# A decoder step on one core: the gate's norm on VectorE, prompt queries and keys in groups of four token tiles, and the latents of two quads loaded later

## The chip, the core and the metric

The kernel runs on one core of a Trainium2 chip, as one launch. The metric is the device time of an execution in microseconds. Matmuls run on TensorE (PE), with weight loads shown apart (PEld); the other engines are VectorE (DVE), ScalarE (ACT), GpSimd (POOL) and SyncE (SP), which issues nearly all the DMAs.

## What is computed

One layer of a hybrid decoder, for a prompt of 1024 tokens and for 8 samples of 4 tokens each whose past of 4096 tokens lies in pages. The part that the change touches:

```python
u, v, cq, ckv, kpe = split_in(rms_norm(xp, g_mix) @ w_in)
# the gate: layer norm over 64 channels, then a causal 128x128 matrix per group
vg = layer_norm(gelu(v).reshape(n, t // c, c, 8, 64), ln_g, ln_b)
a_out = gelu(u) * (einsum('gts,nmsgd->nmtgd', w, vg) + b_s)
# queries and keys of the prompt: 8 heads of 64 + 32 rotated channels
q = qk_rope(rms_norm((rms_norm(cq, g_q_a) @ w_uq).reshape(n, t, 8, 96), g_qk_q), pos)
k = qk_rope(rms_norm(concat([ckv_n @ w_uk, kpe], -1), g_qk_k), pos)
b_out = masked_attend(q, k, ckv_n @ w_uv)
# the samples do the same against their paged latents
xp = xp + concat([rms_norm(a_out), rms_norm(b_out)], -1) @ w_o
```

Cross-attention into 256 memory tokens and a gated ConvFFN follow. All is in fp32.

## The kernel before

The 1056 token rows (1024 of the prompt, 32 of the samples) are nine tiles: 0 to 7 of 128 rows, and 8 of 32. Every fp32 product is made of three matmuls on a high and a low part (`mm3`, L180); `split` (L187) makes the parts, the high one by a cast on ACT and the low one by a subtraction on DVE (L191, L192, and L195, L198 with a gain). `rsqrt_steps` (L216 to L236) is a chain of 11 small DVE operations.

The stages, with their times in the profiled execution:

- *Phase 1, 0 to about 181 us.* The combined projection, in two halves of 256 channels. In each half the gate's values go through gelu on ACT (L457), mean, squares and `rsqrt` on DVE, then three products: by the reciprocal root on DVE (L468), and by the gain and plus the bias on POOL (L470, L472, and L475 for the samples' tile). The result is split into `vgh` and `vgl`, from which TensorE makes the gate. `wsc` (L410) is a copy of a corner of the gate's matrices. The latents `cq` and `ckv` follow in three column groups (`ckr` is the raw latent, `ckh` and `ckl` its parts; `ck_tok`, L576, holds the row scale), and `mix` normalises two tiles of the gate's output at a time, transposes them (L1540), copies them from PSUM (L1541) and stores them (L1543).
- *Projections, about 181 to 209.* `phase2a` first makes tables of cosines and sines times gains, and the rotated shared key `kr`, on POOL (`rope_tables`, `rope_tok`). Then `proj_group` makes queries, keys and values of the first four heads, two tiles at a time: copies and squares on ACT (L842 to L848, the values at L838), the norm on DVE (L849 to L862), the rotation of the queries on POOL (L600 to L603), the product of the keys with their norm on DVE (L871) and of the shared rotated part on POOL (L872). The squares' tiles are `hsq`, the norms `hr`.
- *Attention of the prompt, about 209 to 428.* `head_prep` transposes a head's queries and keys (L895) into `tp` and splits them into `kTh`, `kTl`, `qTh`, `qTl`. `head_unit` does scores (`s`), the eviction with mask and maximum on DVE (L922, L926, tile `pr` or `prs`), the exponential on ACT (L932), transposes (L941), a copy on ACT (`pth`, L943) and the product with the values (L953). The second four heads' projections are spread between these units: `late` groups with the steps given at L692 to L696. POOL sums weights in between (L793 to L796). Three `mix` steps of the attention's output run near the end (L716 to L731); their copies go into tiles of the ring `v`.
- *Samples, about 430 to 875.* Eight batches of eight quads, a quad being four pages. `quad_load` (L1226) reads page numbers into SP's registers and issues four DMAs of `cT` (the latents transposed, with the rope key; L1241; here called the quad's keys) and four of `ck` (the latents by token; L1245). `cT` has three buffers, `ck` fifteen. Quads 0 to 2 get their `cT` during the attention, and their `ck` at the start of this stage. `quad_rot` (L1258 to L1260) rotates the key on POOL; `ch` (ACT) and `cl` (POOL or DVE, L1273) are the parts. `quad_sums` squares the rope part of `ck`. `steps` (L1139) places all this by a counter n, two per quad.
- *From about 875:* keys and values of the memory, the output projection, memory attention, and from 1185 the ConvFFN.

What sets the order: up to the attention a scheduler orders each engine's instructions when the program is built; from the attention on, the order of PE, ACT, DVE and POOL is that of the code (`manual_schedule`). Each engine runs its instructions in order, so an instruction that waits holds up all behind it. SP's queue is in order as well.

## Time and profile before

| | us |
|---|---|
| three runs | 1867.88, 1870.19, 1870.91 |
| median of the runs | 1870.19 |
| the profiled execution | 1868.82 |
| its span | 1867.1 |
| TensorE busy | 1822.4 |
| TensorE idle over the span | 44.7 |

A row of the waits view names the engine and the instruction that waited, then what released it, then the total, the count and the longest. A row of a timeline has the start, the duration, the engine, the line, the operation, the tiles with their shapes, and in brackets the idle time before it and what ended that. A time in brackets on a row of several instructions belongs to the first.

### The profile page before, as it was taken

The page shows a single profiled execution, that of the slowest core. Times are in us where ns is not written, and L with a number is a line of the kernel's source. Part 1 is how long each engine was busy: PE and PEld are TensorE (multiplying, and loading weights), DVE is VectorE, ACT ScalarE, POOL GpSimd, SP SyncE. Part 2 cuts the span into 40 slices and gives each one's busy share as a digit, 9 for nine tenths or more (in the row PEclk, how much of TensorE's full clock was granted, in tenths as well). Part 3 has the DMA queues.
Part 4 walks back from the last instruction along what each step waited for, and adds up shares of the span by engine and source line. Part 5 has one row for each costly group of instructions (what it writes and reads, how often), then busy time and mean ns, then how long its engine had stood idle before and what let it go on. Part 6 is the DMA issues. An engine that isn't in the chain of part 4 may idle for free.

```text
span 1867.1 us, 39819 instructions
## 1 busy us (share of the span) xinstructions
PE 1822.4 (98%) x14414; PEld 1754.4 (94%) x14414; DVE 1376.8 (74%) x2873; ACT 927.6 (50%) x1965; POOL 712.1 (38%) x826
## 2 busy tenths in 40 slices
PE   9999899989999999999999999999999999999999
PEld 8899799889999999998899988899999999999999
DVE  7855967765777667876644676888888888879664
ACT  7335676666556555555533456533323333344442
POOL 1321415643444444543313110267776677500000
PEclk9999899999999999999999999999999999999999
DMA  8002205566776666664554345412222222495252
GB/s 329 29 15 78 68 1 193 205 228 185 220 207 189 175 177 189 170 177 147 163 165 130 127 159 157 136 58 86 76 92 81 69 79 71 117 349 170 75 154 76
DMA packets 133639, 260.18 MB, mean 139 GB/s; under 512 B 20545, under 2 KB 74658, under 8 KB 130370
## 3 DMA queue, kind: packets, MB, share of 16 engines
q1 hardware_dynamic: 132578, 256.58, 44.1%
q8 instruction: 114, 1.87, 0.4%
q10 hardware_dynamic: 864, 1.05, 0.2%
q14 instruction: 83, 0.68, 0.1%
HBM read 212.27 MB, written 45.30 MB: 138 GB/s over the span
## 4 chain that ended last, share of the span: by engine, by line
PE 64%; issue 4%; DVE 3%; DMA 2%; POOL 2%; SPq 1%; ACT 1%; POOLq 0%; DVEq 0%; ACTq 0%
PE s L185 14%; PE d L185 12%; PE b L185 7%; PE X L185 7%; PE F L185 7%; PE E L185 7%; PE A L185 3%; PE y L185 3%; DMA cT<-cT 1%; PE o L1388 1%; SPq L1241 1%; PE t L185 1%; POOL cl L1273 1%; DMA ck<-ck 1%; DVE ss L1316 1%
## 5 line engine op out<-in xcount | busy, mean ns | idle before, releaser
L185 PE MATMUL s<-w2h,ch 128*128 128x288 f32 (+1 forms) x1024 | 304.3, 297 | 0.0
L185 PE MATMUL s<-w2h,cl 128*128 128x288 f32 (+1 forms) x1024 | 296.6, 290 | 3.6 <-POOL cl L1273 3.6
L185 PE MATMUL s<-w2l,ch 128*128 128x288 f32 (+1 forms) x1024 | 295.3, 288 | 0.0
L185 PEld LDWEIGHTS s<-w2h,ch 128*128 128x128 f32 x1024 | 193.2, 189 | 8.3 <-issue 2.9
L185 PEld LDWEIGHTS s<-w2h,cl 128*128 128x128 f32 x1024 | 193.1, 189 | 5.5 <-POOL cl L1273 5.4
L185 PEld LDWEIGHTS s<-w2l,ch 128*128 128x128 f32 x1024 | 193.5, 189 | 0.0
L1316 DVE TENSOR_REDUCE ss<-sq 128x16 f32<-128x1024 f32 x128 | 155.3, 1214 | 34.0 <-ACT sq L1313 33.6
L1273 POOL TENSOR_TENSOR cl<-cT,ch 128x512 fp32r<-128x512 f32 x64 | 83.3, 1301 | 113.9 <-ACT ch L1269 101.6
L1313 ACT ACTIVATE sq<-s 128x512 f32<-128x512 f32 x128 | 76.5, 598 | 91.5 <-PE s L185 91.4
L1310 ACT ACTIVATE sq<-s 128x512 f32<-128x512 f32 x128 | 76.7, 599 | 72.6 <-PE s L185 72.2
L191 ACT CAST a<-brb 128x528 fp32r<-128x528 f32 x77 | 48.9, 635 | 110.7 <-PE d L185 105.4
L192 DVE TENSOR_TENSOR a<-brb,a 128x528 fp32r<-128x528 f32 x77 | 54.2, 706 | 56.7 <-ACT a L191 56.6
L185 PE MATMUL d<-a,w 128*128 128x264 f32 x768 | 95.4, 284 | 0.4 <-DVE G L2108 0.4
L185 PEld LDWEIGHTS d<-a,w 128*128 128x128 f32 x768 | 94.3, 188 | 0.6 <-issue 0.6
L953 PEld LDWEIGHTS o<-v,pth 128*128 128x128 f32 x576 | 75.8, 197 | 7.4 <-ACT pth L943 5.2
L953 PE MATMUL o<-v,pth 128*128 128x64 f32 x576 | 76.2, 274 | 4.8 <-ACT pth L943 4.4
L1979 POOL TENSOR_TENSOR lo<-s,hi 128x1024 fp32r<-128x1024 f32 x20 | 62.9, 3143 | 45.7 <-ACT hi L1978 45.7
L185 PE MATMUL mm<-whi,xh 128*128 128x256 f32 (+3 forms) x272 | 77.9, 288 | 0.0
L185 PE MATMUL mm<-wlo,xh 128*128 128x256 f32 (+3 forms) x272 | 77.7, 288 | 0.0
L185 PE MATMUL mm<-whi,xl 128*128 128x256 f32 (+3 forms) x272 | 77.3, 288 | 0.0
L2034 ACT COPY a<-A 128x264 f32<-128x264 f32 x43 | 16.1, 375 | 118.8 <-PE A L185 113.9
L1269 ACT CAST ch<-cT 128x512 fp32r<-128x512 f32 x128 | 73.4, 626 | 0.8 <-DMA cT<-cT 0.8
(737 smaller groups left out, 6480.6 us busy)
## 6 DMA issues: line engine op xcount, KB each, us to landing
cT<-cT SPq DMA_DIRECT2D x256, 160.0 KB, 2.8
ck<-ck SPq DMA_DIRECT2D x256, 144.0 KB, 3.5
raw<-w_up SPq DMA_DIRECT2D x44, 512.0 KB, 3.6
wsumd<-wsum SPq DMA_DIRECT2D x13, 1024.0 KB, 4.5
actd<-cv SPq DMA_DIRECT2D x44, 264.0 KB, 2.4
brb<-actd SPq DMA_DIRECT2D x44, 264.0 KB, 5.7
wsum<-w_down SPq DMA_DIRECT2D x11, 1024.0 KB, 4.8
raw<-wsumd SPq DMA_DIRECT2D x20, 512.0 KB, 3.8
```

Source lines behind the costliest of these rows:

```text
L185: self.nc.tensor.matmul(out, l, r, start=first and i == 0, stop=last and i == len(seq) - 1)
L191: {"act": nc.scalar.copy, "pool": nc.gpsimd.tensor_copy, "dve": nc.vector.tensor_copy}[eng](hi, src)
L192: low = lambda: nc.vector.tensor_tensor(lo, src, hi, ALU.subtract)
L953: nc.tensor.matmul(u["o"][:, e], th[:, z * P : z * P + P], s["v"][:, jj, h % 4], start=j == z == 0, stop=e == 1 and jj == 2 * G + 1)
L1241: dmas.append([nc.sync.dma_start(cT[:, j], I["cT"][bass.ds(rv, 1)].rearrange("a p n -> (a p) n")) for j, rv in enumerate(rvs)])
L1269: nc.scalar.copy(d["h"][:, k], src[k])
L1273: (nc.vector if k else nc.gpsimd).tensor_tensor(d["l"][:, k], src[k], d["h"][:, k], ALU.subtract)
L1310: nc.scalar.activation(sq[:, 0], ps[:, :, n0 : n0 + 256], AF.Square)
L1313: nc.scalar.activation(sq[:, 1], pt.rearrange("p (e d) -> p e d", e=2), AF.Square)
L1316: yield lambda: nc.vector.tensor_reduce(s["ss"][:, g0 : g0 + 2].rearrange("p e (z h) -> p z e h", z=2), sq.rearrange("p z e (h d) -> p z e ...
L1388: nc.tensor.matmul(s["o"][j * 32 : j * 32 + 32], S[:, q * 4 + j], d["ck"][:, j, :257], start=q == 0 and j > 0, stop=q == 7)
L1979: eng.tensor_tensor(lo, src, hi, ALU.subtract)
```

## The change

1. Gate's norm: the copy at L410 and the products at L470, L472 and L475 go from POOL to DVE.
2. `mix` in phase 1 takes four tiles at a time (0 to 3 in one group; 4 to 7 and 8 in the next), scales the tile in place, and stores two tiles with one DMA. The three `mix` steps of the attention use tiles of the rings `k` and `q` instead of `v`.
3. The tables, the squares of the shared key and its rotation become `rope_setup`, called in phase 1 ahead of the loads of `w_uq`; `rope_tables` goes away.
4. `proj_group` runs on groups (0,4), (4,8), (8,9). Its norm works on four tiles at once; the rotation still goes by pairs. The pieces of the three groups are emitted in a new interleaving, and the late groups have other steps.
5. In `steps`, `ck` of quad 0 is loaded at n = -6, `ck` of quads 1 and 2 at n = 1 and n = 3, behind the loads of quads 3 and 4. `quad_sums` of quads 1 and 2 comes three steps later.

```diff
-            nc.gpsimd.tensor_copy(wsc, ws[:, :, :ND])
+            nc.vector.tensor_copy(wsc, ws[:, :, :ND])
...
-                    nc.gpsimd.tensor_tensor(gf, gf, lng[:tn, c0 : c0 + 256], ALU.mult)
+                    nc.vector.tensor_tensor(gf, gf, lng[:tn, c0 : c0 + 256], ALU.mult)
                     if i < 8:
-                        nc.gpsimd.tensor_tensor(gf, gf, lnb[:tn, c0 : c0 + 256], ALU.add)
+                        nc.vector.tensor_tensor(gf, gf, lnb[:tn, c0 : c0 + 256], ALU.add)
...
+        self.rope_setup(pl, lat)
...
-            for i0 in ((0, 2), (4, 6), (8,))[c]:
+            for i0 in ((0,), (4, 8), ())[c]:
                 mix(i0)
...
-        groups = ((0, 2), (2, 4), (4, 6), (6, 8), (8, 9))
-        for g in groups:
-            for f in sum(self.proj_group(p, pp, 0, *g, st[0], c, ("mm", 5)), []):
-                f()
+        groups = ((0, 4), (4, 8), (8, 9))
+        gs = [self.proj_group(p, pp, 0, *g, st[0], c, ("mm", 5)) for g in groups]
+        (qk, v), (qk1, v1), (qk2, _) = gs
+        for f in qk + v + qk1[:5] + v1[:2] + qk1[5:9] + qk2[:3] + qk1[9:] + v1[2:] + qk2[3:]:
+            f()
...
-        for (q, _), t in zip(late, ((16, 20), (18, 23), (21, 26), (24, 29))):
+        for (q, _), t in zip(late, ((16, 23), (21, 29))):
             spread(q, *t)
...
-                hl = [hl[:, :, a : a + P] for a in (0, P)]
-                nt = lambda j: self.t(p, [P, 2, 4, 96], F32, "k", 4).rearrange("p m h d -> p (m h d)")[:, :512]
+                n = self.t(p, [P, 4, 4, 96], F32, ring, 2).rearrange("p m h d -> p (m h d)")
+                hl = n[:, 512:].rearrange("p (k n) -> p k n", k=4)
...
-            mixes = {28: 0, 29: 2, 30: 1}
+            mixes = {28: (0, "k"), 29: (2, "q"), 30: (1, "k")}
...
-            r = self.t(p, [P, 2, 2, 4], F32, "hr", 2)[:tn, :m]
-            kk = self.t(p, [P, 2, 4, 96], F32, "k", 4)[:tn, :m] if i0 < 8 else None
+            r = self.t(p, [P, 4, 2, 4], F32, "hr", 2)[:tn, :m]
+            kk = self.t(p, [P, 4, 4, 96], F32, "k", 2) if i0 < 8 else None
...
-                if n % 2 == 0 and 0 <= Q + AHEAD < NB * 8:
-                    quads[Q + AHEAD] = self.quad_load(p, Q + AHEAD, quads.get(Q + AHEAD))
+                if n >= 0 and n % 2 == 0 and Q + AHEAD < NB * 8:
+                    quads[Q + AHEAD] = self.quad_load(p, Q + AHEAD)
+                if n in (-6, 1, 3):
+                    k = max(0, n // 2 + 1)
+                    self.quad_load(p, k, quads[k])
...
-                    at(n + 3, 0, self.quad_sums, Q + 1, quads[Q + 1], st[(Q + 1) // 8])
+                    at(n + (6 if 0 <= Q < 2 else 3), 0, self.quad_sums, Q + 1, quads[Q + 1], st[(Q + 1) // 8])
```

How it moves instructions, at three places. Each row has the line, the operation, the tiles written and read, and the shape.

First place: ACT in phase 1, around the last casts of the gate's first half (`vgh`). `gv_656` holds tiles 6 and 7, `gv_698` the samples' tile, `mm_882` and `mm_908` are the last two projections before the gate, and `whi` and `wlo` are the parts of the next weights. Before:

```order
L191 CAST vgh_396<-gv_527 128x256 x3
L486 ACTIVATE a_all_90<-mm_882,rs_tok_67 128x256
L457 ACTIVATE gv_698<-mm_581,rs_tok_67 32x256
L191 CAST vgh_396<-gv_656 128x256
L462 ACTIVATE gsq_705<-gv_698 32x256
L191 CAST vgh_396<-gv_656 128x256
L486 ACTIVATE a_all_90<-mm_908,rs_tok_67 32x256
L191 CAST whi_963<-wraw_523 128x1152 x2
```

The same place in the change:

```order
L486 ACTIVATE a_all_90<-mm_882,rs_tok_67 128x256
L191 CAST vgh_396<-gv_527 128x256
L457 ACTIVATE gv_698<-mm_581,rs_tok_67 32x256
L486 ACTIVATE a_all_90<-mm_908,rs_tok_67 32x256
L191 CAST whi_963<-wraw_523 128x1152 x2
L462 ACTIVATE gsq_705<-gv_698 32x256
L191 CAST vgh_396<-gv_656 128x256 x2
L457 ACTIVATE gv_975<-mm_978,rs_tok_67 128x256
```

The casts of tiles 6 and 7 have moved behind the eviction of `mm_908` and behind both casts of `whi`. On DVE the change has there:

```order
L468 TENSOR_TENSOR gv_656<-gv_656,rv_658 128x256 x2
L470 TENSOR_TENSOR gv_656<-gv_656,rows_231 128x256 x2
L192 TENSOR_TENSOR wlo_964<-wraw_523,whi_963 128x1152
L472 TENSOR_TENSOR gv_656<-gv_656,rows_231 128x256 x2
L192 TENSOR_TENSOR wlo_964<-wraw_523,whi_963 128x1152
```

L470 and L472 are new on DVE, and the first half of `wlo` stands between them.

Second place: DVE at the start of the attention, around the last keys (`k_2727`, tiles 6 and 7) and the first half of the transposed keys (`kTl`). Before:

```order
L236 SCALAR_TENSOR_TENSOR hr_2726<-rqh_402_2781,rqy_403_2782 128x16
L192 TENSOR_TENSOR kTl_2880<-tp_2881,kTh_2879 96x512
L233 TENSOR_TENSOR rqa_417_2850<-rqy_416_2849 32x8
L862 TENSOR_TENSOR rq_2443<-hr_2726,sq_tok_68 128x2x4
L871 TENSOR_TENSOR k_2727<-k_2727,hr_2726 128x8x64
L198 SCALAR_TENSOR_TENSOR qTl_2896<-tp_2897,ggq_2421,qTh_2895 96x512
```

In the change, where `k_2573` holds tiles 4 to 7:

```order
L192 TENSOR_TENSOR kTl_2796<-tp_2797,kTh_2795 96x512
L236 SCALAR_TENSOR_TENSOR hr_2572<-rqh_382_2715,rqy_383_2716 128x32
L234 TENSOR_TENSOR rqa_394_2766<-rqa_394_2766,rqx_391_2763 32x8
L863 TENSOR_TENSOR rq_2407<-hr_2572,sq_tok_68 128x4x4
L875 TENSOR_TENSOR k_2573<-k_2573,hr_2572 128x16x64
L235 SCALAR_TENSOR_TENSOR rqh_392_2764<-rqa_394_2766 32x8
```

The last step of the norm (`hr`) stands behind `kTl` now, where it stood ahead of it, and the product that follows is twice as long.

Third place: PE at the end of the attention, where `o` is the product with the values, `tp<-ident` transposes of the mix, and L1288 (L1295 in the change) the first score of the samples. Before:

```order
L953 MATMUL o_5671<-v_2913,pth_5693 128x64 x4
L1540 MATMUL tp_5713<-ident_60,k_5621 128x128 x4
L1540 MATMUL tp_5720<-ident_60,k_5623 128x128 x4
L953 MATMUL o_5671<-v_2913,pth_5704 128x64 x3
L1288 MATMUL s_5927<-bd_4497,krq_5869 128x128
```

In the change:

```order
L957 MATMUL o_5533<-v_2829,pth_5547 128x64 x4
L1548 MATMUL tp_5567<-ident_60,b_all_2389 128x128 x4
L1548 MATMUL tp_5574<-ident_60,b_all_2389 128x128 x4
L957 MATMUL o_5533<-v_2829,pth_5558 128x64 x3
L1548 MATMUL tp_5585<-ident_60,b_all_2389 128x128 x4
L1295 MATMUL s_5703<-bd_4365,krq_5687 128x128
```

One group of four transposes now stands behind the last product with the values, directly ahead of the samples' first score.

## The prediction

> **What bounds the kernel now.** I read the page's busy times first, then a table of stretches cut at the places that the change touches, then the waits of TensorE. In the table each row is a stretch with its length, the busy time of each engine, and the granted clock (PEclk).

> ```profile
> span 1867.1 us, 39819 instructions
> PE 1822.4 (98%) x14414; PEld 1754.4 (94%) x14414; DVE 1376.8 (74%) x2873; ACT 927.6 (50%) x1965; POOL 712.1 (38%) x826
> ...
> core 0: us, PE busy (x) PEld busy (x) DVE busy (x) ACT busy (x) POOL busy (x), PEclk, DMA share, GB/s
> 0.00:72.00 72.00, 66.25 (x484) 60.48 (x485) 58.09 (x167) 45.02 (x88) 18.11 (x23) 0.98 0.60 224
> 72.00:180.00 108.00, 108.00 (x782) 106.09 (x781) 64.58 (x231) 43.48 (x97) 22.12 (x26) 1.00 0.11 33
> 180.00:224.00 44.00, 35.86 (x233) 32.44 (x231) 41.38 (x157) 29.14 (x133) 25.54 (x49) 0.88 0.33 102
> 224.00:408.00 184.00, 178.55 (x1353) 167.91 (x1353) 129.96 (x446) 127.45 (x347) 79.46 (x83) 0.98 0.42 148
> 408.00:436.00 28.00, 21.42 (x144) 20.81 (x143) 12.26 (x44) 15.49 (x34) 11.92 (x16) 0.82 0.58 178
> 436.00:478.00 42.00, 42.00 (x337) 42.00 (x337) 30.26 (x58) 26.37 (x60) 14.39 (x22) 1.00 0.74 204
> 478.00:510.00 32.00, 30.21 (x237) 29.42 (x236) 27.04 (x54) 18.85 (x41) 18.87 (x28) 1.00 0.76 209
> 510.00:1868.00 1358.00, 1340.11 (x10857) 1295.22 (x10856) 1013.22 (x1723) 621.85 (x1168) 521.70 (x581) 1.00 0.46 139
> ```

> TensorE is the bound in every stretch, and its work is not changed. So the change can only win or lose at the places where TensorE is idle, and in the clock that is lost after such a place. Idle time: 72 - 66.25 = 5.8 us up to 72, nothing from 72 to 180, 44 - 35.86 = 8.1 in 180:224, 184 - 178.55 = 5.5 in 224:408, 28 - 21.42 = 6.6 in 408:436, 32 - 30.21 = 1.8 in 478:510. Lost clock, length times (1 - PEclk): 1.4, 0, 5.3, 3.7, 5.0 and 0 us. Behind 510 nothing is edited. All of this together would be some 43 us; the waits say how much of it the edits reach.

> ```profile
> engine line waited for: us in total, times, longest us
> PE s L185 <- DVE pr L926: 5.2, 8, 2.1
> PE o L953 <- ACT pth L943: 4.4, 1, 4.4
> PE mm L185 <- ACT vgh L191: 3.7, 1, 3.7
> PE s L185 <- POOL cl L1273: 3.6, 8, 1.2
> PE s L185 <- DVE kTl L192: 2.7, 1, 2.7
> ...
> PE s L1288 <- POOL krq L1260: 1.9, 1, 1.9
> ...
> PE tp L895 <- DVE k L871: 1.5, 1, 1.5
> ...
> PE mm L185 <- ACT hsq L846: 1.4, 1, 1.4
> ...
> PE st L283 <- DVE ck_tok L576: 1.0, 1, 1.0
> ...
> PE tp L895 <- POOL k L872: 0.8, 1, 0.8
> PE s L185 <- ACT qTh L195: 0.7, 1, 0.7
> ```

> **A. The gate's norm on VectorE.** Rows of POOL, ACT, DVE and PE around the wait of 3.7 us for the last casts of the gate's values:

> ```profile
> 59.59 1.66 POOL L470 TENSOR_TENSOR gv<-gv,rows 128x256 f32<-128x256 f32 x2 [1.23 <-DVE gv L468]
> 61.20 1.77 POOL L472 TENSOR_TENSOR gv<-gv,rows 128x256 f32<-128x256 f32 x2
> ...
> 64.38 0.39 ACT L191 CAST vgh<-gv 128x256 fp32r<-128x256 f32 x1
> 64.68 0.46 ACT L486 ACTIVATE a_all<-mm,rs_tok 32x256 f32<-32x256 f32 x1
> 65.05 2.19 ACT L191 CAST whi<-wraw 128x1152 fp32r<-128x1152 f32 x2
> ...
> 64.85 0.40 DVE L192 TENSOR_TENSOR vgl<-gv,vgh 128x256 fp32r<-128x256 f32 x1
> ...
> 66.22 1.36 DVE L192 TENSOR_TENSOR wlo<-wraw,whi 128x1152 fp32r<-128x1152 f32 x1
> ...
> 64.82 1.19 PE L185 MATMUL mm<-vgh,wsh 128*128 128x512 f32 x4 [3.73 <-ACT vgh L191]
> ```

> For tiles 6 and 7 POOL takes 1.66 + 1.77 = 3.4 us; four operations of that shape on DVE cost 4 x 0.40 = 1.6 at most (the row of the same size). Read alone, that would end the wait some 2 to 4 us earlier. But the order on ACT and DVE moves too. Before, the casts of tiles 6 and 7 stand ahead of the split of the next weights (whi, wlo); now they stand behind it, and on DVE one half of that split stands between L470 and L472. whi cannot start before TensorE has done with the buffer, at the end of the projections, 64.82 - 3.73 = 61.1. From there: L486 0.46, first half of whi 2.19 / 2 = 1.1, wlo 1.36, two L472 0.8, last vgh 0.39: 61.1 + 4.1 = 65.2, against 64.8 before. So the wait stays at about 4 us, only with another cause. Queued behind on ACT are the first evictions of the next projections; they wait in both versions. I take **0**. Bounds: -5.1 (the 3.7 and the lost clock of 1.4 go) and +0.5.

> **B. Projections and the start of attention, 180:224.** The table of cosines and the rotated keys move to the stretch before, where POOL is busy 22 of 108 us and TensorE never waits: no cost there. Here DVE is busy 41.4 of 44, so what it sheds counts. Of five groups three are left: two norm chains of some 15 small operations less, and the tables' burst on POOL is gone.

> ```profile
> 199.81 0.43 ACT L191 CAST ckh<-ckr 128x288 fp32r<-128x288 f32 x1 [4.84 <-DVE ckr L580]
> ...
> 279.85 0.17 DVE L235 SCALAR_TENSOR_TENSOR rqh<-rqa 128x16 f32<-128x16 f32 x1
> ...
> 215.17 1.68 POOL L872 TENSOR_TENSOR k<-kr,hr 128x256 f32<-128x256 f32 x1 [3.83 <-DVE hr L236]
> ...
> 215.69 0.67 DVE L871 TENSOR_TENSOR k<-k,hr 128x512 f32<-128x512 f32 x1
> ```

> ACT stood 4.84 us before the split of the last latents, waiting for DVE, with the evictions of the projections queued behind it; that is where TensorE's 1.0 (ck_tok) and 1.4 (hsq) come from. About 30 small operations at 0.17 are 5 us of DVE, and TensorE now has three more projections to do ahead of those transposes. I let both waits go: -2.4 (bounds -2.4 and 0). Then comes the hand-over to attention, 2.7 + 1.5 + 0.8 + 0.7 = 5.7 us of waits. The keys of tiles 0 to 3 are ready in time now (1.5 goes). The second half is later relative to the end of the projections: one norm for tiles 4 to 7 has to be through, its product on DVE is twice as long (2 x 0.67 = 1.3), POOL's too (2 x 0.62 to 2 x 1.68), and in DVE's order it stands behind the split of the first half of the transposed keys, which waits for ACT. I reckon 6.4 in place of 5.7, so +0.7 (bounds -2 and +3.4, both products at their contended length). The lost clock of 5.3 should fall with the idle time, 2.4 - 0.7 of 8.1, about -0.8 with rounding down. **B: -2.5**, bounds -6 and +1.5.

> **C. Attention, 224:408.** The only waits are the eight for the score evictions (pr), 5.2 us in all. The second half's groups fall from four to two. 30 small operations less again; the lumps that remain are larger and sit where a row showed trouble:

> ```profile
> 301.90 1.57 DVE L871 TENSOR_TENSOR k<-k,hr 128x512 f32<-128x512 f32 x1
> ```

> This one came in ahead of the longest wait (2.1) while POOL summed weights: 1.57 for what took 0.67 above. Its successor is twice as large, 1.3 to 3.1, but stands one eviction earlier in DVE's order, and one whole chain ahead of it is gone. I take **-1.5**, from the 5.2 and the 3.7 of clock. Bounds -4 (most of the waits and part of the clock) and +3 (two lumps, each 1.57 longer).

> [...]

> **D. The end of attention, 408:436.** The wait of 4.4 (pth) is in ACT's order, which the change leaves: it stays. The 1.9 is put down to POOL, but the POOL result was there earlier; what came last is this:

> ```profile
> 428.40 1.29 DVE L1541 COPY v<-tp 128x512 f32<-128x512 f32 x2 [3.48 <-DMA mix<-v]
> ```

> The copies of the last mix wait 3.48 us for a buffer that an earlier store still reads, and hold the PSUM that the next stage needs. The new code takes its buffers from the rings of queries and keys, so no copy waits for a store. Now the last four transposes stand behind the last values' matmuls, and one copy of 0.65 plus the way there and back is left: about 0.9 in place of 1.9, -1.0. Of the lost clock of 5.0 some falls away, since a wait this short sets off no half-clock stretch where one of 1.9 did: -1.2. **D: -2.2**, bounds -3.5 and +0.5.

> **E. Quads' loads, 436:510.**

> ```profile
> 430.33 8.54 SPq L1245 DMA_DIRECT2D ck<-ck  x12
> 440.51 1.99 SPq L1241 DMA_DIRECT2D cT<-cT  x4
> ```

> SP issues twelve ck loads (8.54 us) and only then quad 3's keys. Now quad 3's keys stand behind four of them, some 5 us earlier; quad 4's keys gain about 3, and from quad 5 on the sum of issues ahead is the same. No wait of TensorE lies in 436:478, so this frees nothing there; the 1.8 in 478:510 comes from POOL's cl after late keys. The sums of quads 1 and 2 are put three steps later, so ACT does not stand in front of a load. **E: -0.8**, bounds -1.8 and +1.5.

> **Sum.** 0 - 2.5 - 1.5 - 2.2 - 0.8 = -7.0. The profiled execution took 1868.82 (span 1867.1, 1.7 around it); less 7.0 is 1861.8. The median of the runs shown is 1870.19, 1.4 above the profiled one, so I predict **1863**.

> **The rivals.**
> 1. The gate's wait goes after all (A at its low bound), because the cast of the weights can start before the projections end, and B and D come at their low sides: -7 - 5 = about 1858, down to 1854. For it: four DVE operations replace 3.4 us of POOL. Against it: the order above.
> 2. The waits change places. DVE is at 94% in 180:224, so what leaves the projections returns at the hand-over, and C's lumps give back what the chains saved; D and E remain in part: about -2, 1868.
> 3. Slower: the groups of four are the mechanism. Tile 4's keys now wait for tile 7's norm; B's hand-over costs +3.4, with a half-clock stretch of 3.4 more that loses 1.5, C costs +3, less D and E (-3.0) and the projections' -2.4 kept only half: +3.4 + 1.5 + 3 - 3 - 1.2 = +3.7, 1874. It decides once the doubled products run at their contended length (3.1, not 1.3).

> [...]

> **Chances.** The sum as it stands 0.45, its own range 1859 to 1867; rival 1 0.18; rival 2 0.22; rival 3 0.15. A measurement of this kernel tells 0.2%, 3.7 us, from no change: faster is below 1866.5, slower above 1873.9. Faster: 0.40 of the first, all of rival 1, 0.05 of rival 2: 0.63. Slower: 0.11 of rival 3 and 0.01 of rival 2: 0.12. Same: the rest, 0.25. All costs at their bounds would span -20 to +7; since they do not fall on one side together, I take 1855 to 1873.

> **What would show it.** A: TensorE still stands 3.5 to 4.5 us near 61, and the row ahead on DVE is wlo, not POOL. B: no wait for ck_tok or hsq; the hand-over waits sum to 5 to 7 us. C: waits for pr between 2 and 6 us. D: 4.4 for pth remains, the wait at the first L1288 falls below 1.2, and PEclk of that stretch rises above 0.82. E: cT of quad 3 issued within 6 us of the first ck. I am wrong if the hand-over exceeds 8 us, if pr exceeds 7, if TensorE waits between 72 and 180, or if anything behind 510 differs by more than 1 us.

## The result and the profile after

The changed kernel takes 1866.78 us (median of 14 runs, 1863.65 to 1871.42) against 1869.09 us for the kernel before on the same chip (14 runs, 1863.98 to 1871.82). The ratio is 0.9991, 95% interval 0.9981 to 1.0001. A second series of the changed kernel, run later beside the experiments, gave 0.9982 (0.9970 to 0.9995). Weighted by runs the two make 0.9987, some 2.4 us less: below the 0.2% (3.7 us) that the prediction took for a difference that can be told.

The profiled execution took 1869.48 us, by chance 0.66 more than that of before. The head of its page, and the table of the same stretches as in the prediction (stretch, length, busy time and instructions of each engine, PEclk, DMA share, GB/s):

```profile
span 1867.6 us, 39666 instructions
PE 1823.0 (98%) x14414; PEld 1754.7 (94%) x14414; DVE 1355.3 (73%) x2824; ACT 928.1 (50%) x1965; POOL 679.1 (36%) x784
```

```profile
0.00:72.00 72.00, 65.98 (x471) 59.65 (x472) 56.31 (x186) 44.76 (x88) 1.74 (x6) 0.95 0.64 234
72.00:180.00 108.00, 108.00 (x777) 105.74 (x777) 63.40 (x234) 44.43 (x100) 13.74 (x23) 1.00 0.08 25
180.00:224.00 44.00, 37.89 (x251) 35.18 (x249) 33.53 (x114) 29.24 (x129) 18.22 (x32) 0.88 0.32 106
224.00:408.00 184.00, 179.01 (x1360) 168.34 (x1360) 121.05 (x417) 127.51 (x347) 80.30 (x79) 0.98 0.42 152
408.00:436.00 28.00, 22.38 (x152) 21.93 (x152) 10.05 (x38) 14.30 (x32) 9.57 (x15) 0.76 0.40 131
436.00:478.00 42.00, 38.34 (x301) 37.72 (x300) 30.12 (x56) 25.74 (x60) 14.62 (x22) 1.00 0.74 201
478.00:510.00 32.00, 30.29 (x239) 29.64 (x238) 26.07 (x55) 18.89 (x40) 18.58 (x25) 1.00 0.77 220
```

DVE lost 21.5 us of work and POOL 33, and TensorE's busy time is the same. In 180:224 DVE fell from 41.4 to 33.5 us and TensorE's idle time from 8.1 to 6.1, but the clock stayed at 0.88. In 0:72 and 408:436 the clock is lower (0.95 for 0.98, 0.76 for 0.82). In 436:478 there are 3.7 us of idle time where there were none. The waits of TensorE, with the total, the count and the longest:

```profile
PE tp L899 <- DVE rqh L235: 5.9, 1, 5.9
PE s L185 <- DVE pr L930: 4.6, 8, 2.1
PE o L957 <- ACT pth L947: 4.6, 1, 4.6
PE mm L185 <- ACT vgh L191: 4.1, 1, 4.1
...
PE s L1295 <- POOL krq L1267: 3.3, 2, 2.7
...
PE s L1295 <- DVE k L1549: 1.0, 1, 1.0
```

The waits for `ck_tok` (1.0), `hsq` (1.4) and the four at the hand-over (2.7, 1.5, 0.8, 0.7) are gone. One wait of 5.9 us stands in their place: four small waits became one large one.

**The account by stage.** A single execution is a poor measure here, so the table takes every profile whose code in that stage is that of the change (the experiments that edit other places count too), and for before its own profile and that of experiment 2, which edits only the loads. Marks are the starts of TensorE's instructions; the hundredth product with the values is counted from zero.

| stage, from mark to mark | before, us | the change: mean (lowest to highest), profiles | difference | predicted |
|---|---|---|---|---|
| A: start to the first product with `vgh` | 64.82, 65.05 | 65.61 (64.98 to 66.27), 8 | +0.7 | 0 |
| from there to the last product of the latents | 115.70, 116.52 | 115.83 (115.05 to 116.35), 8 | -0.3 | 0 |
| B: from there to the last projection | 27.95, 27.55 | 25.19 (all alike), 9 | -2.6 | -2.4 |
| B: from there to the hundredth product with the values | 47.55, 47.56 | 48.81 (46.88 to 50.80), 8 | +1.3 | +0.7 - 0.8 |
| C: from there to the last score of the prompt | 149.46, 149.12 | 148.52 (147.26 to 149.70), 7 | -0.8 | -1.5 |
| D: from there to the samples' first score | 24.36, 25.03 | 24.51 (22.92 to 26.45), 9 | -0.2 | -2.2 |
| E: from there to the samples' 25th score | 77.82 | 78.76 (77.68 to 80.52), 11 | +0.9 | -0.8 |

The differences sum to -0.9 us; with a scatter of 1 to 4 us in most stages that agrees with the -2.4 of the medians. What was gained ahead of the attention is the same in every profile (25.19 us). Half of it was given back at the hand-over, and C, D and E brought less than forecast.

### The profile page after: what moved, and what is told of

It reads as the page before. It is cut to its first block, busy times and chain, and to the rows that moved or that the text cites. A ratio compares the mean times of both kernels' runs of the same rounds, so it can differ in the third digit from the quotient of the medians.

```text
span 1867.6 us, 39666 instructions
## 1 busy us (share of the span) xinstructions
PE 1823.0 (98%) x14414; PEld 1754.7 (94%) x14414; DVE 1355.3 (73%) x2824; ACT 928.1 (50%) x1965; POOL 679.1 (36%) x784
## 3 DMA queue, kind: packets, MB, share of 16 engines
q10 hardware_dynamic: 864, 1.05, 0.2%
## 4 chain that ended last, share of the span: by engine, by line
PE 81%; issue 5%; DMA 4%; DVE 4%; SPq 3%; ACT 2%; POOL 2%; DVEq 0%; POOLq 0%; ACTq 0%
PE s L185 15%; PE d L185 12%; PE mm L185 9%; PE F L185 7%; PE b L185 7%; PE X L185 7%; PE E L185 7%; PE A L185 3%; PE o L957 3%; PE y L185 3%; PE tp L945 1%; SPq L1248 1%; DMA cT<-cT 1%; PE o L1395 1%; DMA ck<-ck 1%
## 5 line engine op out<-in xcount | busy, mean ns | idle before, releaser
L185 PE MATMUL s<-w2h,ch 128*128 128x288 f32 (+1 forms) x1024 | 303.8, 297 | 0.3 <-DVE S L1319 0.3
L185 PE MATMUL s<-w2h,cl 128*128 128x288 f32 (+1 forms) x1024 | 295.8, 289 | 3.5 <-POOL cl L1280 3.5
L185 PE MATMUL s<-w2l,ch 128*128 128x288 f32 (+1 forms) x1024 | 294.6, 288 | 0.0
L185 PEld LDWEIGHTS s<-w2h,ch 128*128 128x128 f32 x1024 | 192.6, 188 | 8.8 <-issue 2.5
L185 PEld LDWEIGHTS s<-w2h,cl 128*128 128x128 f32 x1024 | 192.4, 188 | 5.3 <-POOL cl L1280 5.3
L185 PEld LDWEIGHTS s<-w2l,ch 128*128 128x128 f32 x1024 | 192.8, 188 | 0.0
L191 ACT CAST a<-brb 128x528 fp32r<-128x528 f32 x77 | 48.8, 634 | 110.6 <-PE d L185 107.3
L192 DVE TENSOR_TENSOR a<-brb,a 128x528 fp32r<-128x528 f32 x77 | 54.3, 707 | 57.4 <-ACT a L191 57.2
L185 PE MATMUL d<-a,w 128*128 128x264 f32 x768 | 95.4, 284 | 0.4 <-DVE G L2117 0.4
L185 PEld LDWEIGHTS d<-a,w 128*128 128x128 f32 x768 | 94.3, 188 | 0.6 <-issue 0.6
L185 PE MATMUL mm<-whi,xh 128*128 128x256 f32 (+3 forms) x272 | 78.2, 288 | 0.0
L185 PE MATMUL mm<-wlo,xh 128*128 128x256 f32 (+3 forms) x272 | 77.5, 287 | 0.0
L185 PE MATMUL mm<-whi,xl 128*128 128x256 f32 (+3 forms) x272 | 77.4, 288 | 0.0
```

The source lines that it names most:

```text
L185: self.nc.tensor.matmul(out, l, r, start=first and i == 0, stop=last and i == len(seq) - 1)
L191: {"act": nc.scalar.copy, "pool": nc.gpsimd.tensor_copy, "dve": nc.vector.tensor_copy}[eng](hi, src)
L192: low = lambda: nc.vector.tensor_tensor(lo, src, hi, ALU.subtract)
```

## The experiments

All diffs are against the changed kernel, but for the second.

**1 and 2. The loads alone (E).** The trace after had a wait that the kernel before did not have, 2.74 us for `krq` at 462. The first kernel undoes only the edit to the loads:

```diff
-                if n >= 0 and n % 2 == 0 and Q + AHEAD < NB * 8:
-                    quads[Q + AHEAD] = self.quad_load(p, Q + AHEAD)
-                if n in (-6, 1, 3):
-                    k = max(0, n // 2 + 1)
-                    self.quad_load(p, k, quads[k])
+                if n % 2 == 0 and 0 <= Q + AHEAD < NB * 8:
+                    quads[Q + AHEAD] = self.quad_load(p, Q + AHEAD, quads.get(Q + AHEAD))
...
-                    at(n + (6 if 0 <= Q < 2 else 3), 0, self.quad_sums, ...)
+                    at(n + 3, 0, self.quad_sums, ...)
```

> The changed kernel with part 5 (the order of the quads' loads and the later sums) put back as it was before. Theory: the deferral of the two quads' latents is a loss of its own; in the profile of the change TensorE waits 2.7 + 0.6 us for krq near 462 and 476, which the kernel before did not have, and the samples' stage falls 3.7 us behind between their first score and the fourth quad pair. Then this run has no wait for krq above 1.2 us, loses nothing between the first samples' score and 510, and its ratio to the kernel before is about 0.997 (the change alone 0.9991). Rival, the prediction's own term E: the loads as changed gain 0.8 us, and the late krq comes from something else; then the ratio is 0.9991 or higher and the waits for krq stay.

The second makes the same edit the other way round, in the kernel before:

> The kernel before with part 5 alone. Theory: it costs 3 to 4 us, ratio 1.0015 to 1.002, with waits for krq of 2 to 4 us between 436 and 480. Rival: ratio 0.9996 (a gain of 0.8 us) and no wait for krq. A third way: SyncE's queue in the kernel before starts these loads at another point, and the cost needs the earlier finish of the attention; then the ratio is 1.000 within 0.001.

Measured: 0.9997 (0.9985 to 1.0010) and 0.9996 (0.9986 to 1.0005), both to the kernel before. The stage E took 78.02 us with the old order in the new kernel and 78.34 with the new order in the old one, against 77.82 before. SP's queue in the changed kernel, with start and duration:

```profile
431.02 2.33 SPq L1252 DMA_DIRECT2D ck<-ck  x4
434.48 1.92 SPq L1248 DMA_DIRECT2D cT<-cT  x4
436.59 6.94 SPq L1252 DMA_DIRECT2D ck<-ck  x8
445.23 2.28 SPq L1248 DMA_DIRECT2D cT<-cT  x4
447.72 6.52 SPq L1252 DMA_DIRECT2D ck<-ck  x8
455.94 0.89 SPq L1248 DMA_DIRECT2D cT<-cT  x2
```

and with the old order in the same kernel:

```profile
432.22 8.11 SPq L1249 DMA_DIRECT2D ck<-ck  x12
441.98 1.92 SPq L1245 DMA_DIRECT2D cT<-cT  x4
...
454.27 2.46 SPq L1245 DMA_DIRECT2D cT<-cT  x4
```

Quad 3's keys come 3.5 us behind the first `ck` instead of 9.8. Quad 5's come 24.9 us behind it instead of 22.1: the eight `ck` of two quads took 6.94 and 6.52 us where twelve in one go took 8.11, so 5.4 for eight. The edit moves the late keys from quad 3 to quad 5: with the old order TensorE stood 1.14 us for `krq` at 448, with the new one 0.96 to 2.74 us for `krq` in six of eleven profiles; the kernel before, with the old order, did not wait there at all. The theory that the loads cost the change 3 us falls. The gain of 0.8 us that the prediction gave them (0.9996) can be neither shown nor excluded with these intervals.

**3. The gate's norm back on GpSimd (A).**

```diff
-            nc.vector.tensor_copy(wsc, ws[:, :, :ND])
+            nc.gpsimd.tensor_copy(wsc, ws[:, :, :ND])
...
-                    nc.vector.tensor_tensor(gf, gf, lng[:tn, c0 : c0 + 256], ALU.mult)
+                    nc.gpsimd.tensor_tensor(gf, gf, lng[:tn, c0 : c0 + 256], ALU.mult)
...
-                        nc.vector.tensor_tensor(gf, gf, lnb[:tn, c0 : c0 + 256], ALU.add)
+                        nc.gpsimd.tensor_tensor(gf, gf, lnb[:tn, c0 : c0 + 256], ALU.add)
...
```

> The changed kernel with the gate's norm products (and the small copy of the gate's matrices) put back on GpSimd. The prediction's term A: worth nothing; TensorE stands 3.5 to 4.3 us near 61 to 66 in both, ratio as the change alone within 0.0007. Rival: the products on VectorE are worth 1 to 2 us by easing VectorE's small operations further on; then the ratio is 1.000. Other rival: the new order there costs more than it saves; then the ratio is 0.998 and the wait is below 3.5.

Measured: 0.9992 (0.9979 to 1.0006), and a wait for `vgh` of 4.4 us instead of 4.1. The norm's engine is worth 0.3 us of that wait and nothing that can be told in the time.

**4. The late groups in pairs (C).** Four groups of two tiles with their old steps, in the buffers of the change:

```diff
-        late = [self.proj_group(p, pp, 1, *g, st[1], c) for g in groups]
-        for (q, _), t in zip(late, ((16, 23), (21, 29))):
+        late = [self.proj_group(p, pp, 1, *g, st[1], c) for g in ((0, 2), (2, 4), (4, 6), (6, 8), (8, 9))]
+        for (q, _), t in zip(late, ((16, 20), (18, 23), (21, 26), (24, 29))):
             spread(q, *t)
...
```

> The changed kernel with the late groups (second four heads, during the attention) in pairs of tiles again with their old steps; the first half stays in groups of four. Theory: the groups of four are worth about 1 us between 224 and 408 (waits for pr 4.6 instead of 5.2, and the first late chain no longer delays evictions), so this run is about 1 us slower than the change, ratio 0.9996. Rival: larger lumps cost as much as they save; ratio as the change, 0.9991 or lower, waits for pr no larger than 4.6.

Measured: 0.9992 (0.9980 to 1.0005); the waits for `pr` sum to 4.9 us with the same longest one, 2.1. Groups of four in the second half bring nothing that can be told, and the longest wait is not theirs.

**5. The changed kernel again, unedited.**

> The changed kernel once more, unedited: a control for what one profiled execution shows. The first profile of it had waits of 2.7 and 0.6 us for krq near 462 and 476; two other kernels with the same order of loads had one of 0.96 and 0.97. If the loss in the samples' stage is the loads' own, the waits come back at 2 us or more and the stretch from the first samples' score to the thirteenth quad pair takes some 80 us again; if it was that execution's DMAs, the stretch takes 77.7 to 78.3 as in the four experiments and 77.8 as in the kernel before. Ratio 0.998 to 1.000 either way.

Measured: 0.9982 (0.9970 to 0.9995). The wait of 2.7 us for `krq` is not there; the longest for it in that stage is 0.3. It differs from execution to execution (2.2 in experiment 6). The distance of this series to the first (0.0009) is what the other ratios have to be read by: the edits below are compared with 0.9987, the mean of the two.

**6. Half of the hand-over in pairs (B).** Tiles 4 to 7 of the first four heads as two groups of two, in one shared tile; tiles 0 to 3 stay together:

```diff
-        gs = [self.proj_group(p, pp, 0, *g, st[0], c, ("mm", 5)) for g in groups]
-        (qk, v), (qk1, v1), (qk2, _) = gs
-        for f in qk + v + qk1[:5] + v1[:2] + qk1[5:9] + qk2[:3] + qk1[9:] + v1[2:] + qk2[3:]:
+        early = ((0, 4), (4, 6), (6, 8), (8, 9))
+        gs = [self.proj_group(p, pp, 0, *g, st[0], c, ("mm", 5)) for g in early]
+        (qk, v), (qa, va), (qb, vb), (qk2, _) = gs
+        for f in qk + v + qa[:5] + qa[5:] + va + qb[:5] + qk2[:3] + qb[5:] + vb + qk2[3:]:
             f()
...
```

> The changed kernel with tiles 4 to 7 of the first four heads in two groups of two, so that the last norm ahead of the first scores covers two tiles. Theory: the one wait of 5.9 us at the hand-over is the four-tile norm and its doubled products on VectorE and GpSimd; with pairs the wait falls by 1.5 to 2.5 us, the half-clock stretch behind it gets shorter at times, and the stretch from the last projection to steady attention is 1.5 to 4 us shorter; ratio about 0.9985. Rival: the wait is set by the order on ScalarE and VectorE (split of the first half of the keys, the sample tile's chain), whatever the group's size; then it stays at 5 to 6 us and the ratio is as the change.

Measured: 0.9961 (0.9947 to 0.9975), 1861.56 us, in 7 runs. The wait is 4.0 us, and 46.05 us pass to the hundredth product with the values. DVE there in the changed kernel, and POOL beside it:

```profile
211.32 0.67 DVE L192 TENSOR_TENSOR kTl<-tp,kTh 96x512 fp32r<-96x512 f32 x1
211.93 0.17 DVE L236 SCALAR_TENSOR_TENSOR hr<-rqh,rqy 128x32 f32<-128x32 f32 x1
...
212.22 1.22 DVE L875 TENSOR_TENSOR k<-k,hr 128x1024 f32<-128x1024 f32 x1
213.35 1.00 DVE L235 SCALAR_TENSOR_TENSOR rqh<-rqa 32x8 f32<-32x8 f32 x1
```

```profile
212.24 2.10 POOL L876 TENSOR_TENSOR k<-kr,hr 128x512 f32<-128x512 f32 x1 [5.38 <-DVE rqa L234]
```

and in this experiment:

```profile
210.82 0.68 DVE L880 TENSOR_TENSOR k<-k,hr 128x512 f32<-128x512 f32 x1
211.42 0.57 DVE L235 SCALAR_TENSOR_TENSOR rqh<-rqa 32x8 f32<-32x8 f32 x1
211.92 0.67 DVE L192 TENSOR_TENSOR kTl<-tp,kTh 96x512 fp32r<-96x512 f32 x1
```

TensorE goes on when POOL has written the shared part of the last keys (212.24 + 2.10 = 214.34, TensorE 214.40), though the row names DVE. In pairs the norm is ready before `kTl`, POOL's piece is half as long (1.13 us), and the wait 1.9 us shorter. Of the single edits it is the one whose interval lies wholly below that of the first series of the change (0.9981 to 1.0001), and it shares 0.0005 with that of the second; on the same chip the medians are 1861.56 against 1865.85 us. What it undoes is the part of the change that cost. The edit also gives the pieces a new order: TensorE has two more transposes of the keys and eight of the queries to do ahead of the wait. No run parts the size of the groups from that order.

**7. The gate's casts ahead of the weights' (A).** An order edge puts the first cast of `whi` behind the last cast of `vgh`:

```diff
...
+                if name == "u1":
+                    tc.add_manual_dep(
+                        self.high.ins, self.gate.ins.name,
+                        mybir.DependencyInfo(mybir.DependencyClass.NoSync, mybir.DependencyReason.DATA), reason="order",
+                    )
...
```

> The changed kernel with the casts of the next weights held behind the last casts of the gate's values on ScalarE (an order alone, no wait added). Theory (the prediction's term A): the norm on VectorE would end TensorE's wait earlier but for the weights' split in between. Then the wait at the gate falls from 4.1 to about 2.7 us (the first half of wlo, 1.36, no longer stands between the two products) and the half-clock stretch may get 3.4 us shorter; ratio about 0.9982. Rival: the chain of small operations on VectorE ends late by itself, so the wait falls by less than 0.5 us.

Measured: 0.9978 (0.9965 to 0.9990); the wait for `vgh` is 3.1 us, not 4.1. The order held 1 us of it; what is left is the norm's own chain on DVE, for whose last operation ACT waits 1.55 us. The ratio can't be told from 0.9987.

**8. The mixes one unit later (D).**

```diff
-            mixes = {28: (0, "k"), 29: (2, "q"), 30: (1, "k")}
+            mixes = {29: (0, "k"), 30: (2, "q"), 31: (1, "k")}
```

> The changed kernel with each of the three mix steps at the end of the attention started one result later. Theory: the wait of 4.6 us for pth comes from the mix's scaling and squares standing ahead of that copy on ScalarE; started later, the wait falls by 1 to 2 us (squares of 1.2 us no longer ahead of it), but the last mix stands nearer to the samples' first score, where the wait of 1.0 us grows to 2 to 3; ratio as the change within 0.001. Rival: the wait for pth is set by the last scores' maximum on VectorE and the exponentials, not by the mix; then it stays above 4 and the other grows, ratio 1.000 or above.

Measured: 0.9976 (0.9963 to 0.9988). Its waits of that stage:

```profile
PE o L957 <- ACT pth L947: 3.1, 2, 1.7
PE tp L1548 <- ACT b_all L1541: 2.7, 1, 2.7
```

The 4.6 us became 1.5 and 1.7, and a new wait of 2.7 came for the last mix. From the last score of the prompt to the first of the samples it is 23.33 us, inside the scatter of the nine profiles of D, and the ratio can't be told from 0.9987. The wait moves rather than goes.

**9. Unused matmuls in the gap (the clock at the hand-over).** 24 matmuls of 128x512 whose result nothing reads stand in the place of the wait:

```diff
-        for f in self.head_prep(pm, pp, 0, st[0], c):
+        for x, f in enumerate(self.head_prep(pm, pp, 0, st[0], c)):
             f()
+            if x == 0:
+                d = self.t(pp, [P, 512], F32, "tp", 4)
+                for _ in range(24):
+                    nc.tensor.matmul(d, self.ckh[:, 0, :P], self.ckh[:, 0, :512], start=True, stop=True)
```

> The changed kernel with 24 matmuls of 128x512 into a PSUM tile that nothing reads, placed at the hand-over behind the first transposes of the keys, where TensorE otherwise waits 5.9 us. Theory: the wait itself is the smaller part of what the hand-over costs; the half-clock stretch that follows it was 3.4, 10.2 and 17.1 us long in executions of the same code, which makes the stretch from the last projection to the hundredth value product 46.9, 48.2 or 50.6 us. With TensorE kept busy there is no such stretch: that part takes about 46 us in every execution, although no work is removed, and the ratio is about 0.9970 (the change 0.9987 over its two measurements). Rival: the clock falls anyway or the extra matmuls delay the transposes; then that part takes 48 or more and the ratio is 0.9987 or above.

Measured: 0.9991 (0.9979 to 1.0003). The stretches there:

```profile
205.00:213.20 8.20, 7.80 (x46) 6.50 (x45) 7.50 (x32) 4.34 (x22) 2.25 (x2) 1.00 0.48 185
213.20:216.60 3.40, 2.24 (x17) 1.65 (x14) 3.26 (x12) 1.74 (x3) 1.45 (x4) 1.00 0.00 0
216.60:226.80 10.20, 10.20 (x36) 9.29 (x37) 6.43 (x22) 5.19 (x13) 0.00 (x0) 0.50 0.00 1
```

The long wait is filled and none that is left there exceeds 0.64 us, yet half clock came at 216.6, behind a stretch in which TensorE was busy 2.24 of 3.40 us, and lasted 10.2 us in which TensorE was busy throughout. To the hundredth product with the values 50.2 us pass, as the rival had it (48 or more). That filling this one wait keeps the clock is refuted; whether the clock would stay with the last 1.16 us filled too, no run shows.

**10. Head 4's preparation one step later (C).**

```diff
-        spread(self.head_prep(pm, pp, 4, st[1], c), 29, 33)
+        spread(self.head_prep(pm, pp, 4, st[1], c), 30, 34)
```

> The changed kernel with the transposes of head 4 (its keys and queries) spread one step later (30 to 34 instead of 29 to 33). Theory: the longest wait for pr, 2.1 us near 304, which stood unchanged in every kernel so far, has nothing to do with the groups' products that the prediction blamed; VectorE stands 1.4 us idle there for the cast of head 4's keys on ScalarE, with the evictions behind it. Then the wait of 2.1 falls below 0.8 and with it the half-clock stretch of 6.8 us at 305; ratio 0.0005 to 0.0015 below the change. Rival: the doubled product on VectorE sets it; then it stays at about 2.

Measured: 0.9969 (0.9955 to 0.9984), 1863.47 us. The wait of 2.1 us is gone and C takes 145.53 us, 1.7 below the lowest profile of the change. The ratio is 0.0018 below 0.9987, about 3 us, but its interval overlaps with those of the changed kernel, so the time alone does not tell it. The stretch 295:310 in the changed kernel:

```profile
295.00:310.00 15.00, 12.93 (x83) 12.38 (x83) 10.30 (x31) 5.39 (x14) 11.42 (x13) 0.81 0.80 278
```

and with the later step:

```profile
295.00:310.00 15.00, 14.78 (x113) 13.82 (x113) 11.78 (x36) 9.48 (x23) 12.51 (x12) 1.00 0.74 269
```

TensorE's idle time there falls from 2.07 to 0.22 us, and with it goes the lost clock of 15 x 0.19 = 2.9 us.

**11. The hand-over, the gate's order and the mixes together** (diffs of 6, 7 and 8).

> Three edits together: tiles 4 to 7 of the first heads in pairs, the next weights' casts behind the gate's, the mix one result later. If each keeps its worth (hand-over wait 4.0, gate wait 3.2, waits for pth 1.7 and less), the ratio is 0.994 to 0.9955. If they only move the same half-clock stretches about, it is that of the pairs alone, 0.996 or above.

Measured: 0.9967 (0.9952 to 0.9982), in 8 runs: the second expectation. All three waits shrink as they did alone, but its profile has a half-clock stretch at 362 that no other kernel here has (PEclk 0.62 in 365:375), and C took 152.86 us.

**12. The hand-over, the gate's order and head 4's step together** (diffs of 6, 7 and 10).

> Three edits of which each alone read faster, put together: the first heads' tiles four to seven as two groups of two, the gate's first cast behind the last cast of the gate's values, and head 4's preparation one step later per piece. If the waits decide, the gate's wait is about 3.1 us, the hand-over's about 4.0 (or 2.9 and 1.0), the wait of 2.1 us near 300 is gone, and the ratio to before lies between 0.9935 and 0.9955. If gains at separate places do not add (as they did not with the three edits of the run before), because a half-clock stretch appears or lengthens elsewhere, the ratio is 0.996 or above.

Measured: 0.9958 (0.9945 to 0.9972), 1859.97 us (1857.31 to 1861.01), in 6 runs. Its waits, the first as in the changed kernel:

```profile
PE o L968 <- ACT pth L958: 4.6, 1, 4.6
PE s L185 <- DVE pr L941: 3.6, 7, 1.2
...
PE mm L185 <- ACT vgh L191: 3.1, 1, 3.1
PE s L185 <- ACT qTh L195: 2.9, 1, 2.9
```

The waits are as expected, and C takes 145.29 us. The ratio lies between the two expectations and its interval covers both, so whether the gains add stays open. It is faster than the kernel before and than the change, and not to be told from the hand-over in pairs alone (0.9961).

## Why the prediction was right or wrong

The time, 1866.8, lies in the range 1855 to 1873 and 4 us above the 1863 forecast. That it would be faster by over 0.2% had a chance of 0.63 and did not come about; "within 0.2%" had 0.25. The range is 18 us wide, so that the time lies in it says little for the sum. The miss is more than those 4 us: the base, 1870.19 from three runs, was 1.1 above the 1869.09 of 14, and of the -7.0 some -2.4 came. The closest of the cases in size is rival 2, the waits change places, about -2; by the stages its mechanism held in part at the hand-over, and not in C.

**A: right.** 0 was forecast, with a wait of 3.5 to 4.5 behind `wlo`. It is 4.10 for 3.73 (the stage +0.7, inside its scatter), and DVE and ACT stand as read from the order:

```profile
63.75 1.36 DVE L192 TENSOR_TENSOR wlo<-wraw,whi 128x1152 fp32r<-128x1152 f32 x1
65.03 0.75 DVE L472 TENSOR_TENSOR gv<-gv,rows 128x256 f32<-128x256 f32 x2
```

```profile
62.59 2.19 ACT L191 CAST whi<-wraw 128x1152 fp32r<-128x1152 f32 x2
...
65.48 0.74 ACT L191 CAST vgh<-gv 128x256 fp32r<-128x256 f32 x2 [0.39 <-DVE gv L472]
```

Experiment 3 confirms it from the other side, and 7 shows that the order held 1 us of it. The clock behind the wait differs between executions of both kernels: up to 72 it is 0.98 before and 0.95 in experiment 2, whose code there is the same, and 0.95 in the changed kernel and 0.98 in experiment 8, whose code there is the same as well.

**B: the mechanism right, the term for what follows mis-sized.** The projections' waits went as forecast (-2.6 for -2.4). The hand-over's wait is 5.9 where 6.4 was reckoned. Wrong was the step "the lost clock of 5.3 should fall with the idle time": PEclk of 180:224 is 0.88 as before, and over eight profiles the time to the hundredth product with the values is 1.3 us longer, not 0.1 shorter. In the three of them that lost as much clock as the kernel before (half clock for 10.24 us) it is 48.2 for 47.55, so the +0.7 of the wait was right, and the -0.8 of the clock did not come. So B brought -1.3, not -2.5. Its upper bound, +1.5, was also too low by its own terms, which allow the hand-over +3.4. Rival 3's mechanism, that tile 4 waits for tile 7, is what experiment 6 undoes, and of the single edits that one gained most. At the hand-over, where DVE was busy 33.5 of 44 us, the smaller pieces, with the order that came with them, took the ratio from 0.9987 to 0.9961; in C (0.9992 in experiment 4) they changed nothing that can be told.

**C: wrong in its cause.** The prediction blamed the product at L871 (1.57 us) for the longest wait. In the changed kernel the product is through long before (299.69, 1.21 us), and the wait is 2.08 as it was. DVE and ACT ahead of it:

```profile
301.54 0.21 DVE L932 TENSOR_SCALAR nm<-nm,rq 128x1 f32<-128x1 f32 x1
303.20 0.69 DVE L192 TENSOR_TENSOR kTl<-tp,kTh 96x512 fp32r<-96x512 f32 x1 [1.44 <-ACT kTh L191]
303.81 0.48 DVE L930 TENSOR_SCALAR_CACHE_REDUCE pr<-s 128x320 f32<-128x320 f32 x1
```

```profile
301.79 0.82 ACT L936 ACTIVATE prs<-prs,nm,rq 128x512 f32<-128x512 f32 x1 [2.94 <-DVE nm L932]
...
302.61 0.56 ACT L191 CAST kTh<-tp 96x512 fp32r<-96x512 f32 x1
```

DVE's next in order is `kTl` of head 4, which needs ACT's `kTh`; that stands on ACT behind an exponential that waits for DVE's `nm`; and the eviction that TensorE waits for stands on DVE behind `kTl`. The same was to be read in the trace before:

```profile
302.84 0.56 ACT L191 CAST kTh<-tp 96x512 fp32r<-96x512 f32 x1
...
303.43 0.69 DVE L192 TENSOR_TENSOR kTl<-tp,kTh 96x512 fp32r<-96x512 f32 x1
```

`kTh` ended at 303.40 there, and `kTl` began at 303.43: the long product only filled a gap that was there without it. Experiment 10 moves `kTh` and `kTl` away from that place, and the wait and its half clock go, in its profile and in that of experiment 12.

**D: the waits right, the clock behind the long one left out.** The wait at the samples' first score fell from 1.85 to 1.04 us, and the long one for `pth` stayed (4.6), both as forecast. That "a wait this short sets off no half-clock stretch" came true at this place; in general it was not shown, for in experiment 9 half clock came behind waits of 0.64 us and less. The stretch behind it, before (a wait of 1.85 us) and after (1.04):

```profile
427.00:440.00 13.00, 11.15 (x78) 10.95 (x77) 5.85 (x11) 5.78 (x14) 5.49 (x9) 0.87 0.89 225
```

```profile
427.00:440.00 13.00, 11.64 (x93) 11.22 (x92) 5.78 (x12) 4.95 (x12) 5.85 (x9) 1.00 0.87 243
```

It is 0.87 in experiment 2 too, and 1.00 in all nine profiles of the change that the table takes for D. What the forecast left out is the clock behind the long wait: in 400:427 it is 0.87 before and 0.81 in experiment 2, and 0.75 to 0.87 in those nine. So PEclk of 408:436 fell from 0.82 to 0.76 in the profile after instead of rising, the stage took 22.9 to 26.5 us, and -0.2 is what is left of the -2.2.

**E: the queue misread, the worth not told.** Quad 3's keys came 3.5 us behind the first `ck`, within the 6 forecast. "From quad 5 on the sum of issues ahead is the same" failed by 2.9 us of SP's time (24.9 for 22.05), and TensorE waited 0.9 us or more for `krq` in six of eleven profiles with the new order and in one of two with the old. The stage is +0.9 against one profile of before; by experiments 1 and 2 its worth in time can't be told from nothing, nor from the -0.8.

As forecast, TensorE waited nowhere between 72 and 180. Behind 510 the trace differed by more than the 1 us allowed (300.20 us before, 298.07 after from the memory's first product to the ConvFFN's), though nothing was edited there; the same stretch took 296.9 to 299.6 us in the twelve other profiles, whose code there is alike. By the prediction's own sign that counts against it, but 1 us was less than the scatter.

## What to carry to other kernels

When work in front of a hand-over is grouped, ask when the last piece of the group is ready and who stands behind it: large groups up to the hand-over and small ones at it gave what large ones everywhere did not. A row with a long duration just ahead of a wait is not its cause until the row behind it has been asked what else it waited for. Count a shortened wait at its own length; the clock that is lost behind it (half clock for 3.41, 10.24 or 17.07 us at the same wait of 5.9 us here) should be counted as a scatter, not as a gain, where the trace has not shown it twice.

## What the runs showed of the hardware

**One wait, three prices.** Eight profiles have the same code at the hand-over and the same wait of 5.86 to 5.88 us. The stretch 205:232 in three of them, experiment 7, the changed kernel and its second series:

```profile
205.00:232.00 27.00, 20.49 (x141) 17.94 (x139) 23.26 (x86) 18.64 (x50) 3.55 (x5) 0.94 0.14 54
```

```profile
205.00:232.00 27.00, 20.89 (x124) 18.22 (x122) 22.21 (x79) 17.39 (x59) 5.33 (x9) 0.81 0.21 78
```

```profile
205.00:232.00 27.00, 21.03 (x105) 18.82 (x104) 21.02 (x75) 15.32 (x44) 3.64 (x6) 0.68 0.14 57
```

| half clock began before the wait's end | it lasted | profiles |
|---|---|---|
| 0.5 and 0.6 us | 3.41 us | experiments 8, 7 |
| 2.3 us | 10.24 us | the change, 4, 10 |
| 2.6, 2.9, 3.0 us | 17.07 us | 1, the second series, 3 |

The hundredth product with the values comes 46.9, 48.2 or 50.6 to 50.8 us in, in these three groups: 3.9 us go with where the grid falls, more than half of what the whole change was forecast to bring. The times of single runs fit: of the 26 runs of the changed kernel, the four with a granted clock of 0.993 took 1862.2 to 1864.0 us and the five with 0.987 or 0.988 took 1867.0 to 1871.4. What brings full clock back the runs do not show: in experiment 9 TensorE was busy 10.20 of 10.20 us, about three of these steps, and stayed at half clock throughout.

**VectorE and GpSimd side by side.** At the hand-over POOL's product of 128x512 started 0.02 us behind DVE's and took 2.10 us; the same product took 1.05 us here:

```profile
298.68 1.05 POOL L876 TENSOR_TENSOR k<-kr,hr 128x512 f32<-128x512 f32 x1 [0.65 <-DVE rsum L962]
```

The difference is about one DVE product of 1.22 us, which itself took no longer beside POOL's than the 1.21 at 299.69. DVE's next operation, `rqh` of 32x8, took 1.00 us and ended at 214.35, with POOL's product (214.34), where the same operation took 0.15 us at 214.96. What made the two take longer, these rows do not show.
